# Sliding-window attention in a two-layer trunk: values as stationary weights in two column tiles, probabilities moving, and the later tokens' two key blocks merged by the mask

## The chip, the cores and the metric

The kernel runs on one core of one Trainium2 chip. The metric is the device time of one execution in microseconds. Three runs of the kernel before gave 2478.45, 2480.82 and 2482.11 us, median 2480.82.

The profile names the engines PE (TensorE; PEld are its weight loads), DVE (VectorE), ACT (ScalarE), POOL (GpSimd) and SP (SyncE, which only issues DMAs here). A q behind a name is that engine's instruction queue.

## What is computed

Two layers over 256 tokens of width 2048, in f32. The attention of each layer has 16 query heads of width 64 in 4 groups, one key and value head per group, a window of 128 tokens and a learned sink per head:

```python
scores = jnp.einsum('bnqhgd,bnkhd->bnhgqk', qb, kw).astype(jnp.float32) * scale
q_pos = jnp.arange(BLOCK)[:, None] + BLOCK
k_pos = jnp.arange(2 * BLOCK)[None, :]
diff = q_pos - k_pos
band = (diff >= 0) & (diff < WINDOW)
...
scores = jnp.where(mask, scores, -1e30)
...
probs = jax.nn.softmax(jnp.concatenate([scores, sink], axis=-1), axis=-1)[..., :-1]
out = jnp.einsum('bnhgqk,bnkhd->bnqhgd', probs.astype(v.dtype), vw)
```

With two blocks of 128 tokens, a query of the first block sees keys of its own block up to itself. A query at place q of the second block sees keys 0 to q of its own block and keys q+1 to 127 of the block before: 128 in all, one for each column of a block. The output of the attention goes through `w_attn_branch` (1024 x 2048). Beside it a spatial gating branch, the gates, an output projection and a feed-forward part (width 5632) make up the layer; their large products take most of the time.

## The kernel before

**Large products.** All weights stream from memory in pieces of 256 rows and 512 columns (`Stream`, lines 180 to 230), through five buffers `raw`. ScalarE copies a piece into a rounded part `whi` (line 221), VectorE subtracts to get the rest `wlo` (line 222). Activations are kept the same way as a pair `uh`, `ul`, with features on the partitions. A product is then three matmuls: `whi` by `uh`, `wlo` by `uh`, `whi` by `ul` (lines 309, 310, 311, in `add_product`), each with a 128x128 stationary block of activations and 512 moving columns of weights. For most column pairs (`pair`) a quarter of the rows is done with seven block products for eight, from sums of weights and of activations, which adds work on VectorE (lines 209, 335).

**The order of the work.** TensorE's order is the program's. Small work such as the attention is put between large products: `after(n, fn)` registers a step, `tick()` runs the steps that are due, once per 12 large matmuls. Inside a step the instructions of the other engines are queued behind the latest `wlo` that was issued. VectorE's and ScalarE's order is chosen when the program is built, by a scheduler; it is fixed at run time, and each engine takes its instructions in that order.

**The attention.** In `FIRST_PART` keys and values (`kv`, 256 columns each) and two column halves of queries (`q`, c = 0 and 1, eight heads each, two groups) are projected. `Attention.rotate` normalises and rotates them; `turn` transposes blocks of 32 on VectorE (line 379) and puts them in place by 16 DMAs (line 384), issued for the attention on SP's queue. For each half c, tile of tokens t and group g:

- `scores` (lines 710 to 741): for each row half j, two f32 matmuls of 64 rows into a bank of `ps_at` (line 719); the mask of 0 and -1e30 is added by VectorE (line 723), over 128 columns per head for t = 0 and 256 for t = 1; maximum (727), exponentials on ScalarE (736) with the sums, `den` (738) and its reciprocal `rd` (740).
- `weights`, five ticks later: TensorE transposes the four heads' probabilities `pr` into a bank of `ps_tr`, one per block of keys (748), and ScalarE copies them out as `pT` (750).
- `values`, three ticks later: for each head and block of keys a matmul with `pT` as the stationary 128x128 block and 64 moving columns of values (758). VectorE multiplies the result by `rd` into `att` (762).

After the last group of a half, `transposed` turns `att` on VectorE and SP, and splits it into `uh` and `ul` for the product with `w_attn_branch`.

**Memory.** Most of these tiles are `slot`s: 25 buffers of 4 KB per partition. `pT` and other short-lived tiles are `temp`s (5 buffers). PSUM has four banks for large sums, two (`ps_tr`) for transposes and two (`ps_at`) shared by scores, values and the spatial branch.

Of the kernel before, what the change touches and what calls it, by code (L numbers as in the profile page):

```python
# [8 lines left out]
F32 = mybir.dt.float32  # L9
# [5 lines left out]
P = 128  # L15
# [42 lines left out]
def hybrid_trunk(ctx: ExitStack, tc: tile.TileContext, x, mix_norm, w_in, q_norm, k_norm, sinks,  # L58
# [92 lines left out]
    plans = []  # L151
    for l in range(DEPTH):
        wl = w_in[l]

        def of_in(kind, c):
            o = {"kv": O_KV, "q": 0, "v": O_V, "u": O_U, "gate": O_GATE}[kind] + c * CW
            return wl[:, o:o + CW]

        for f in FIRST_PART[l]:
            plans.append((single if len(f) == 1 else pair)(("in", l), *(of_in(*c) for c in f)))  # L160
        plans += [single(("att", l), w) for w in cols_of(w_attn_branch[l], NCH)]
# [22 lines left out]
    class Stream:  # L184
# [7 lines left out]
        def load(self, upto):  # L192
            while self.asked < min(upto, len(entries)):
                for key, w, h, tag in entries[self.asked]["loads"]:
                    raw = wraw.tile([P, 2, CW], F32, tag=tag, name=nm("raw"), bufs=None if tag == "raw" else 1)
                    src = w[2 * h * P:2 * (h + 1) * P, :].rearrange("(k p) n -> p k n", p=P)
                    if self.raws:
                        self.loaded = nc.sync.dma_start(raw, src)
                    else:
                        for i in range(2):  # L200
                            self.loaded = nc.sync.dma_start(raw[:, i:i + 1], src[:, i:i + 1])
                    self.raws[key] = raw
                self.asked += 1

# [317 lines left out]
    for c in range(NCH):  # L522
# [6 lines left out]
    nc.gpsimd.affine_select(mask[:, :P], mask[:, :P], pattern=[[1, P]], base=0, channel_multiplier=-1,  # L529
                            compare_op=ALU.is_gt, fill=-1e30)  # L530
    nc.gpsimd.affine_select(mask[:, P:], mask[:, P:], pattern=[[-1, P]], base=0, channel_multiplier=1,
                            compare_op=ALU.is_ge, fill=-1e30)
# [100 lines left out]
    class Attention:  # L633


        def __init__(self, pl):
            self.pl = pl
            self.qT = [None] * 2
            self.att = [None] * 2
            self.attT = [None] * 2  # L640
            self.live = {}

        def rotate(self, src, n, rope, outs):

# [64 lines left out]

        def scores(self, t, g):  # L710
            nk = P * (t + 1)
            mk = mask[:, P:] if t == 0 else mask
            snk, nsnk = self.pl.snk, self.pl.nsnk
            pr = slot([P, 2, 2, S], name="pr")
            for j in range(2):
                pscore = ps_at.tile([P, 2, S], F32, tag="at", name=nm("psc"))
                for i in range(2):
# [5 lines left out]
                nc.vector.tensor_tensor(out=pr[:, :, j, :nk], in0=pscore[:, :, :nk],  # L723
                                        in1=mk.unsqueeze(1).to_broadcast([P, 2, nk]), op=ALU.add)
            pr4 = pr.rearrange("p i j k -> p (i j) k")
            mx = tiny(4, "mx")
            nc.vector.tensor_reduce(out=mx, in_=pr4[:, :, :nk], axis=AX.X, op=ALU.max)
            nm_ = tiny(4, "negm")
            nc.vector.scalar_tensor_tensor(out=nm_, in0=mx, scalar=-1.0, in1=nsnk[:, 4 * g:4 * g + 4],
                                           op0=ALU.mult, op1=ALU.min)  # L730
# [2 lines left out]
            nc.scalar.activation(es, es, AF.Exp)  # L733
            den = tiny(4, "den")
            for h in range(4):
                nc.scalar.activation(pr4[:, h, :nk], pr4[:, h, :nk], AF.Exp, bias=nm_[:, h:h + 1],
                                     accum_out=den[:, h:h + 1])
            nc.vector.tensor_tensor(out=den, in0=den, in1=es, op=ALU.add)
            rd = tiny(4, "rd")
            nc.vector.reciprocal(out=rd, in_=den)  # L740
            after(5, lambda: self.weights(t, g, pr4, rd))

        def weights(self, t, g, pr4, rd):
            pT = []
            for kb in range(t + 1):
                pt = ps_tr.tile([P, 4, P], F32, tag="tr", name=nm("ppt"))
                for h in range(4):
                    nc.tensor.transpose(pt[:, h, :], pr4[:, h, kb * P:(kb + 1) * P], ident)  # L748
                pT_ = temp((P, 4, P), "pT")
                nc.scalar.activation(pT_, pt, AF.Copy)  # L750
                pT.append(pT_)
            after(3, lambda: self.values(t, g, pT, rd))

        def values(self, t, g, pT, rd):
            po = ps_at.tile([P, 4, HD], F32, tag="at", name=nm("po"))
            for h in range(4):
                for kb in range(t + 1):
                    nc.tensor.matmul(po[:, h, :], pT[kb][:, h, :],  # L758
                                     self.kv[:, kb, KVW + g * HD:KVW + (g + 1) * HD],
                                     start=kb == 0, stop=kb == t)  # L760
            o = (g % 2) * 256
            nc.vector.tensor_tensor(out=self.att[g // 2][:, t, o:o + 256].rearrange("p (h d) -> p h d", d=HD),
                                    in0=po, in1=rd.unsqueeze(2).to_broadcast([P, 4, HD]), op=ALU.mult)

    class Spatial:

# [236 lines left out]
```

## Time and profile before

| | |
|---|---|
| time of three runs | 2478.45, 2480.82, 2482.11 us |
| span of the profiled execution | 2481.3 us |
| TensorE busy, share of the span | 2465.4 us, 99% |
| VectorE | 1930.1 us, 78% |
| ScalarE | 1430.9 us, 58% |
| granted TensorE clock in the attention's stretches | 1.00 |
| bytes read from memory | 475.27 MB, 192 GB/s over the span |
| attention on TensorE, instructions of scores, transposes, values | 128, 96, 192 |

The page gives busy time per engine, groups of instructions with count, mean time and what ended the idle time before them, and the chain of waits that ended last. Matmuls overlap: a large one is shown as 0.39 us, but the next starts before it ends, so starts are to be compared and not durations. An f32 matmul is recorded as two instructions, a transpose as one.

The attention of layer 0 lies between about 100 and 250 us (first half c = 0 up to about 185), that of layer 1 between about 1340 and 1490 us.

### The profile page before, as it was taken

How to read it: one execution, taken by the hardware profiler on the slowest of the kernel's cores; microseconds unless marked ns; L12 is line 12 of the kernel's file. 1: busy time of each engine (PE TensorE's matmuls, PEld its weight loads, DVE VectorE, ACT ScalarE, POOL GpSimd, SP SyncE). 2: the span in 40 equal slices, each digit the busy share in tenths (PEclk: the TensorE clock that was granted, in tenths of full speed). 3: DMA queues.
4: the chain of work that ended last, by engine and by line, in shares of the span. 5: the costliest groups of instructions: out<-in, count | busy, mean ns of one | idle time of the engine just before them, and what ended most of it. 6: DMA issues, size and time to landing. Idle time of an engine off the chain costs nothing.

```text
span 2481.3 us, 31298 instructions
## 1 busy us (share of the span) xinstructions
PE 2465.4 (99%) x11088; PEld 2028.1 (82%) x11088; DVE 1930.1 (78%) x2261; ACT 1430.9 (58%) x1794; POOL 283.4 (11%) x527
## 2 busy tenths in 40 slices
PE   9999999999999999999999999999999999999999
PEld 7888888888888888888887888888888888888887
DVE  6698676887877787778887986768878777877786
ACT  5567544575655565556655665546655555655564
POOL 3100002231110111001101000021211001110110
PEclk9999999999999999999999999999999999999999
DMA  8565667576666667576747446666757566666664
GB/s 292 192 190 158 215 197 220 184 234 194 217 198 198 212 191 229 171 225 190 228 147 270 147 159 223 207 209 195 224 188 231 185 214 195 217 197 203 211 191 150
DMA packets 275661, 502.54 MB, mean 203 GB/s; under 512 B 26224, under 2 KB 36048, under 8 KB 275504
## 3 DMA queue, kind: packets, MB, share of 16 engines
q1 hardware_dynamic: 259472, 484.25, 61.3%
q0 software_dynamic: 15712, 16.01, 2.2%
q8 instruction: 87, 1.43, 0.2%
q14 instruction: 70, 0.57, 0.1%
q10 hardware_dynamic: 320, 0.27, 0.0%
HBM read 475.27 MB, written 2.10 MB: 192 GB/s over the span
## 4 chain that ended last, share of the span: by engine, by line
PE 90%; DVE 4%; DMA 2%; issue 1%; SPq 1%; ACT 1%; POOL 0%; DVEq 0%; ACTq 0%
PE acc L309 29%; PE acc L311 29%; PE acc L310 29%; DMA raw<-in_w_in_dram 2%; DVE wlo L222 2%; SPq L384 1%; PE po L758 1%; ACT whi L221 1%; DVE raw L209 1%; PE pt L421 1%; PE ppt L748 0%; PE psc L719 0%; DVE box L379 0%; PE psg L836 0%; DVE ul L412 0%
## 5 line engine op out<-in xcount | busy, mean ns | idle before, releaser
L222 DVE TENSOR_TENSOR wlo<-raw,whi 128x1024 fp32r<-128x1024 f32 (+1 forms) x1039 | 1264.8, 1220 | 498.5 <-ACT whi L221 481.3
L221 ACT ACTIVATE whi<-raw 128x1024 fp32r<-128x1024 f32 (+1 forms) x1039 | 1098.0, 1058 | 929.2 <-PE acc L311 749.3
L309 PE MATMUL acc<-whi,uh 128*128 128x512 f32 x3114 | 1218.1, 391 | 2.5 <-ACT uh L407 1.6
L310 PE MATMUL acc<-wlo,uh 128*128 128x512 f32 x3114 | 1212.9, 390 | 1.7 <-DVE wlo L222 1.6
L311 PE MATMUL acc<-whi,ul 128*128 128x512 f32 x3114 | 1212.8, 389 | 0.0
L310 PEld LDWEIGHTS acc<-wlo,uh 128*128 128x128 f32 x3114 | 585.1, 188 | 124.9 <-DVE wlo L222 4.7
L309 PEld LDWEIGHTS acc<-whi,uh 128*128 128x128 f32 x3114 | 585.1, 188 | 123.6 <-ACT uh L407 1.8
L311 PEld LDWEIGHTS acc<-whi,ul 128*128 128x128 f32 x3114 | 584.8, 188 | 122.5
L384 POOL DMA_DIRECT2D tt<-box x480 | 235.1, 497 | 1716.6 <-DVE box L379 835.7
L209 DVE TENSOR_TENSOR raw<-raw,raw 128x1024 f32<-128x1024 f32 x188 | 229.2, 1219 | 1.3
L309 PE MATMUL acc<-whi,sh 128*128 128x512 f32 x376 | 150.6, 401 | 3.7 <-DVE kept L335 2.8
L311 PE MATMUL acc<-whi,sl 128*128 128x512 f32 x376 | 146.7, 390 | 0.0
L310 PE MATMUL acc<-wlo,sh 128*128 128x512 f32 x376 | 146.5, 390 | 0.0
L309 PEld LDWEIGHTS acc<-whi,sh 128*128 128x128 f32 x376 | 70.5, 188 | 30.2 <-issue 12.3
L311 PEld LDWEIGHTS acc<-whi,sl 128*128 128x128 f32 x376 | 70.6, 188 | 15.1
L310 PEld LDWEIGHTS acc<-wlo,sh 128*128 128x128 f32 x376 | 70.7, 188 | 13.1
L335 DVE TENSOR_TENSOR kept<-acc,kept 128x512 f32<-128x512 f32 x94 | 64.1, 682 | 0.0
L338 ACT ACTIVATE acc<-kept 128x512 f32<-128x512 f32 x94 | 54.0, 587 | 7.5 <-DVE kept L335 7.4
L853 DVE SCALAR_TENSOR_TENSOR xs<-acc,xs 128x512 f32<-128x512 f32 (+1 forms) x66 | 41.2, 666 | 7.8 <-PE acc L311 7.8
L942 ACT ACTIVATE hid<-acc,rhalf 128x512 f32<-128x512 f32 x44 | 30.4, 690 | 21.0 <-PE acc L311 21.0
L332 ACT ACTIVATE kept<-acc 128x512 f32<-128x512 f32 x47 | 28.1, 597 | 15.0 <-PE acc L311 15.0
L943 DVE SCALAR_TENSOR_TENSOR hid<-hid,acc 128x512 f32<-128x512 f32 x44 | 29.6, 683 | 8.3 <-ACT hid L942 8.3
(135 smaller groups left out, 878.5 us busy)
## 6 DMA issues: line engine op xcount, KB each, us to landing
raw<-in_w_in_dram SPq DMA_DIRECT2D x239, 512.0 KB, 4.7
raw<-in_w_up_dram SPq DMA_DIRECT2D x176, 512.0 KB, 4.8
raw<-in_w_gate_dram SPq DMA_DIRECT2D x176, 512.0 KB, 4.6
raw<-in_w_down_dram SPq DMA_DIRECT2D x176, 512.0 KB, 4.7
raw<-in_w_out_dram SPq DMA_DIRECT2D x64, 512.0 KB, 4.9
raw<-in_w_attn_branch_dram SPq DMA_DIRECT2D x32, 512.0 KB, 5.4
raw<-in_w_sgu_branch_dram SPq DMA_DIRECT2D x32, 512.0 KB, 4.4
tt<-box POOLq DMA_DIRECT2D x480, 32.0 KB, 4.2
```

What stands on the lines that cost most here:

```text
L209: self.last = nc.vector.tensor_tensor(out=self.raws[d], in0=self.raws[x], in1=self.raws[y], op=ALU.subtract)
L221: nc.scalar.activation(hi[:, i, :], raw[:, i, :], AF.Copy)
L222: self.last = nc.vector.tensor_tensor(out=lo[:, i, :], in0=raw[:, i, :], in1=hi[:, i, :].bitcast(F32), op=ALU.subtract)
L309: nc.tensor.matmul(ps, a, hi[:, kk, :], start=first and kk == 0, stop=False, skip_group_check=True)
L310: nc.tensor.matmul(ps, a, lo[:, kk, :], start=False, stop=False, skip_group_check=True)
L311: nc.tensor.matmul(ps, b, hi[:, kk, :], start=False, stop=kk == 1, skip_group_check=True)
L335: nc.vector.tensor_tensor(out=p.kept[:, int(tag == "P7"), :], in0=a[1], in1=p.kept[:, 1, :], op=ALU.add)
L338: nc.scalar.activation(ps, p.kept[:, t, :], AF.Copy)
L384: queue.dma_start(dst[j * B:(j + 1) * B, i], box[i * B:(i + 1) * B, j])
L853: nc.vector.scalar_tensor_tensor(out=xs[:, t, sl], in0=sums[t][:, i * w:(i + 1) * w], scalar=scale, in1=xs[:, t, sl], op0=ALU.mult, op1=AL ...
L942: nc.scalar.activation(th, g[t], AF.Tanh, scale=norm.rh[t])
L943: nc.vector.scalar_tensor_tensor(out=th, in0=th, scalar=1.0, in1=g[t], op0=ALU.add, op1=ALU.mult)
```

## The change

1. **Values.** One step per half c and tile of tokens t, in place of one per group. The values of a group (128 keys x 64) are the stationary operand; the turned probabilities of the group's four heads (128 keys x 512) move. The two groups of the half write partitions 0 to 63 and 64 to 127 of one bank. The result has features on partitions already, so the turn of `att` is gone: ScalarE copies the bank to `uh`, VectorE subtracts to get `ul`. The pairs `uh`, `ul` are allocated when the queries of the half begin.
2. **Scaling.** `rd` multiplies the probabilities before they are turned, two ticks after the scores.
3. **Second tile of tokens.** The two blocks of scores are merged into one of 128 columns: ScalarE copies the own block's scores, VectorE overwrites those where the mask is set with the block before's. Maximum, exponentials and transposes run over 128 columns per head instead of 256. The values are V0 times all turned probabilities plus (V1 - V0) times those of the own block, which a 0/1 matrix `causal` selects (V0 the block before). Hence `kv`'s first key columns, which are free after the rotation, are overwritten with V1 - V0.

   In the program's names: for t = 1 and k = 0 the stationary operand is the first block's values, for k = 1 the difference.
4. **Attention-branch weights.** The features of the output now lie in another order, so each load of these weights is made by two DMAs of 64 partitions, from rows picked by head.

```diff
+    def rows_of(raw, w, h):
+
+        if w.shape[0] != QW or not any(w is a for a in by_heads):
+            return [(raw, w[2 * h * P:2 * (h + 1) * P, :].rearrange("(k p) n -> p k n", p=P))]
+        rows = w.rearrange("(c a k d) n -> c a d k n", c=2, a=2, d=HD)
+        k = 2 * (h % 2)
+        return [(raw[a * HD:(a + 1) * HD], rows[h // 2, a, :, k:k + 2]) for a in range(2)]
...
-    mask = const.tile([P, S], F32, name="mask")
+    mask = const.tile([P, P], F32, name="mask")
...
+    causal = const.tile([P, P], F32, name="causal")
+    nc.gpsimd.memset(causal, 1.0)
+    nc.gpsimd.affine_select(causal, causal, pattern=[[1, P]], base=0, channel_multiplier=-1, compare_op=ALU.is_ge, fill=0.0)
...
+            after(K_TURN, lambda: nc.vector.tensor_tensor(out=kv[:, 0, :KVW], in0=kv[:, 1, KVW:], in1=kv[:, 0, KVW:],
+                                                          op=ALU.subtract))
...
-            self.att[c] = slot([P, NT, CW], name="att")
+            self.attT[c] = None
+            units = slot([P, 4, S], F32R, "uh"), slot([P, 4, S], F32R, "ul")
...
                     after(n, lambda t=t, g=g: self.scores(t, g))
                     n += Q_STEP
-            after(n + 6, lambda: transposed(self.attT, c, self.att[c], queue=nc.sync))
+                after(n + 3, lambda t=t: self.values(t, c, units))
...
-            pr = slot([P, 2, 2, S], name="pr")
+            if g % 2 == 0:
+                self.pr[t, g // 2] = slot([P, 2, 4, P], name="pr")
+            pr4 = self.pr[t, g // 2][:, g % 2]
...
-                nc.vector.tensor_tensor(out=pr[:, :, j, :nk], in0=pscore[:, :, :nk],
-                                        in1=mk.unsqueeze(1).to_broadcast([P, 2, nk]), op=ALU.add)
+                mk = mask.unsqueeze(1).to_broadcast([P, 2, P])
+                if t == 0:
+                    nc.vector.tensor_tensor(out=pr[:, :, j, :], in0=pscore[:, :, :P], in1=mk, op=ALU.add)
+                else:
+                    nc.scalar.activation(pr[:, :, j, :], pscore[:, :, P:], AF.Copy)
+                    nc.vector.copy_predicated(pr[:, :, j, :], mk.bitcast(mybir.dt.uint32), pscore[:, :, :P])
...
-            after(5, lambda: self.weights(t, g, pr4, rd))
...
+            after(2, lambda: nc.vector.tensor_tensor(out=pr4, in0=pr4, in1=rd.unsqueeze(2).to_broadcast([P, 4, P]),
+                                                     op=ALU.mult))
+            after(5, lambda: self.weights(t, g, pr4))
+
+        def weights(self, t, g, pr4):
+            if g % 2 == 0:
+                self.pT[t, g // 2] = [slot([P, 2, 4, P], name="pT") for _ in range(t + 1)]
+            pT = self.pT[t, g // 2]
+            pt = ps_tr.tile([P, 4, P], F32, tag="tr", name=nm("ppt"))
             for h in range(4):
...
+                nc.tensor.transpose(pt[:, h, :], pr4[:, h, :], ident)
+            nc.scalar.activation(pT[0][:, g % 2], pt, AF.Copy)
+            if t == 1:
+                nc.vector.tensor_tensor(out=pT[1][:, g % 2], in0=pt, in1=causal.unsqueeze(1).to_broadcast([P, 4, P]),
+                                        op=ALU.mult)
+
+        def values(self, t, c, units):
+            po = ps_at.tile([P, 4, P], F32, tag="at", name=nm("po"))
+            pT = self.pT[t, c]
+            for k in range(t + 1):
+                for a in range(2):
+                    v = (1 - k) * KVW + (2 * c + a) * HD
+                    nc.tensor.matmul(po[a * HD:(a + 1) * HD], self.kv[:, 0, v:v + HD], pT[k][:, a],
+                                     start=k == 0, stop=k == t)
+            uh, ul = (x[:, :, t * P:(t + 1) * P] for x in units)
+            nc.scalar.activation(uh, po, AF.Copy)
+            nc.vector.tensor_tensor(out=ul, in0=po, in1=uh.bitcast(F32), op=ALU.subtract)
+            if t == NT - 1:
+                self.attT[c] = units
```

More of the change, by code (lines that the diff above doesn't have):

```diff
@@ L149, in pair @@
         return Plan(key, head, body)
-    plans = []
+    plans, by_heads = [], []
     for l in range(DEPTH):
@@ L160, in hybrid_trunk @@
             plans.append((single if len(f) == 1 else pair)(("in", l), *(of_in(*c) for c in f)))
-        plans += [single(("att", l), w) for w in cols_of(w_attn_branch[l], NCH)]
+        by_heads += cols_of(w_attn_branch[l], NCH)
+        plans += [single(("att", l), w) for w in by_heads[-NCH:]]
         sgu = [single(("sgu", l), w_sgu_branch[l, :, j * CW:(j + 1) * CW]) for j in range(NCH)]
@@ L195, in load @@
                     raw = wraw.tile([P, 2, CW], F32, tag=tag, name=nm("raw"), bufs=None if tag == "raw" else 1)
[L196 to L201, printed above, removed]
+                    for dst, src in rows_of(raw, w, h):
+                        if self.raws:
+                            self.loaded = nc.sync.dma_start(dst, src)
+                        else:
+                            for i in range(2):
+                                self.loaded = nc.sync.dma_start(dst[:, i:i + 1], src[:, i:i + 1])
                     self.raws[key] = raw
@@ L525, in hybrid_trunk @@
     after(10, lambda: norm.unit(WINO, again=True))
-    mask = const.tile([P, S], F32, name="mask")
+    mask = const.tile([P, P], F32, name="mask")
     nc.gpsimd.memset(mask, 0.0)
-    nc.gpsimd.affine_select(mask[:, :P], mask[:, :P], pattern=[[1, P]], base=0, channel_multiplier=-1,
-                            compare_op=ALU.is_gt, fill=-1e30)
-    nc.gpsimd.affine_select(mask[:, P:], mask[:, P:], pattern=[[-1, P]], base=0, channel_multiplier=1,
+    nc.gpsimd.affine_select(mask, mask, pattern=[[-1, P]], base=0, channel_multiplier=1,
                             compare_op=ALU.is_ge, fill=-1e30)
+    causal = const.tile([P, P], F32, name="causal")
+    nc.gpsimd.memset(causal, 1.0)
+    nc.gpsimd.affine_select(causal, causal, pattern=[[1, P]], base=0, channel_multiplier=-1, compare_op=ALU.is_ge, fill=0.0)
     cs = const.tile([P, NT, HD // 2], F32, name="cs")
@@ L638, in __init__ @@
             self.qT = [None] * 2
-            self.att = [None] * 2
             self.attT = [None] * 2
-            self.live = {}
+            self.pr, self.pT = {}, {}
         def rotate(self, src, n, rope, outs):
@@ L711, in scores @@
             nk = P * (t + 1)
-            mk = mask[:, P:] if t == 0 else mask
             snk, nsnk = self.pl.snk, self.pl.nsnk
-            pr = slot([P, 2, 2, S], name="pr")
+            if g % 2 == 0:
+                self.pr[t, g // 2] = slot([P, 2, 4, P], name="pr")
+            pr4 = self.pr[t, g // 2][:, g % 2]
+            pr = pr4.rearrange("p (i j) k -> p i j k", j=2)
             for j in range(2):
@@ L722, in scores @@
                                      start=True, stop=True)
-                nc.vector.tensor_tensor(out=pr[:, :, j, :nk], in0=pscore[:, :, :nk],
-                                        in1=mk.unsqueeze(1).to_broadcast([P, 2, nk]), op=ALU.add)
-            pr4 = pr.rearrange("p i j k -> p (i j) k")
+                mk = mask.unsqueeze(1).to_broadcast([P, 2, P])
+                if t == 0:
+                    nc.vector.tensor_tensor(out=pr[:, :, j, :], in0=pscore[:, :, :P], in1=mk, op=ALU.add)
+                else:
+                    nc.scalar.activation(pr[:, :, j, :], pscore[:, :, P:], AF.Copy)
+                    nc.vector.copy_predicated(pr[:, :, j, :], mk.bitcast(mybir.dt.uint32), pscore[:, :, :P])
             mx = tiny(4, "mx")
-            nc.vector.tensor_reduce(out=mx, in_=pr4[:, :, :nk], axis=AX.X, op=ALU.max)
+            nc.vector.tensor_reduce(out=mx, in_=pr4, axis=AX.X, op=ALU.max)
             nm_ = tiny(4, "negm")
@@ L735, in scores @@
             for h in range(4):
-                nc.scalar.activation(pr4[:, h, :nk], pr4[:, h, :nk], AF.Exp, bias=nm_[:, h:h + 1],
+                nc.scalar.activation(pr4[:, h, :], pr4[:, h, :], AF.Exp, bias=nm_[:, h:h + 1],
                                      accum_out=den[:, h:h + 1])
@@ L740, in scores @@
             nc.vector.reciprocal(out=rd, in_=den)
-            after(5, lambda: self.weights(t, g, pr4, rd))
[L743 to L752, printed above, removed]
@@ L754, in values @@
-        def values(self, t, g, pT, rd):
-            po = ps_at.tile([P, 4, HD], F32, tag="at", name=nm("po"))
-            for h in range(4):
[L757 to L763, printed above, removed]
+            after(2, lambda: nc.vector.tensor_tensor(out=pr4, in0=pr4, in1=rd.unsqueeze(2).to_broadcast([P, 4, P]),
+                                                     op=ALU.mult))
```

## The prediction

> **What bounds the kernel now.** I read the page's busy shares and costliest groups first, then the order of time on TensorE, then TensorE's waits.
>
> ```profile
> PE 2465.4 (99%) x11088; PEld 2028.1 (82%) x11088; DVE 1930.1 (78%) x2261; ACT 1430.9 (58%) x1794; POOL 283.4 (11%) x527
> ...
> L309 PE MATMUL acc<-whi,uh 128*128 128x512 f32 x3114 | 1218.1, 391 | 2.5 <-ACT uh L407 1.6
> ...
> L309 PE MATMUL acc<-whi,sh 128*128 128x512 f32 x376 | 150.6, 401 | 3.7 <-DVE kept L335 2.8
> ```
> ```profile
> 108.05 0.39 PE L310 MATMUL acc<-wlo,uh 128*128 128x512 f32 x1
> ...
> 117.11 0.39 PE L311 MATMUL acc<-whi,ul 128*128 128x512 f32 x1
> ```
>
> Lines 309, 310 and 311 each run 3114 + 376 times, so 10470 large matmuls. The two timeline rows are 40 starts apart: 9.06 / 40 = 0.2265 us each, and 10470 x 0.2265 = 2371 us of the 2481.3 us span. TensorE is the bound; a microsecond taken from it counts, unless it then waits. VectorE is second, and the table by stretches shows where it binds:
>
> ```profile
> 124.00:170.00 46.00, 44.72 (x229) 36.10 (x230) 45.26 (x85) 33.47 (x62) 3.86 (x2) 1.00 0.59 189
> 170.00:250.00 80.00, 80.00 (x416) 66.41 (x415) 69.09 (x117) 53.35 (x96) 2.61 (x3) 1.00 0.55 166
> 1360.00:1400.00 40.00, 38.47 (x189) 31.16 (x190) 38.94 (x76) 26.95 (x50) 2.02 (x2) 1.00 0.51 163
> ```
>
> Columns: stretch, length, then busy time of TensorE, its weight loads, VectorE, ScalarE, GpSimd, then clock (1.00: full), DMA share, GB/s. In the first column half's attention of each layer (rows one and three) VectorE is busy 45.26 of 46 and 38.94 of 40 us, and of the three rows only these show TensorE idle. In the second half (row two) it has room.
>
> **TensorE's part: what goes.** In the chain of waits stand the prices of the attention's blocks:
>
> ```profile
> 163.91 1.73 PE po L758 x16
> ...
> 188.32 0.65 PE psc L719 x8
> ...
> 196.40 0.84 PE po L758 x8
> 204.13 1.07 PE psc L719 x8
> ...
> 236.71 0.88 PE ppt L748 x8
> ...
> 253.04 0.86 PE psg L836 x4
> ```
>
> Columns: start, time on the chain, work. There are 16 value blocks (2 layers, 4 groups, 2 tiles of tokens): 8 of the first tile at 0.84 and 8 of the second at 1.73, together 20.6 us. The second tile's transposes fall from eight to four in 8 blocks: 8 x 0.44 = 3.5 us gone.
>
> **What comes.** Eight value blocks instead of 16, each of a tile of tokens and a column half: 4 instructions for the first tile, 8 for the second (an f32 matmul is recorded as two), 512 moving columns each. No such instruction is in the trace. The nearest is psg: 0.86 / 4 = 0.215 us for 256 columns, so 0.43 for 512. Two column tiles at once do not occur either; the nearest is psc, whose two row halves do: eight instructions of 256 columns take 1.07, not 8 x 0.215 = 1.72. That is four pairs at 0.215, 0.86, and 0.21 over for entering and leaving (at 128 columns 0.65, by the same rule 0.43 + 0.21). By it a new block costs 2 x 0.43 + 0.21 = 1.07 or 4 x 0.43 + 0.21 = 1.93, and eight cost 4 x 3.00 = 12.0. I take this row because it is the same kind of split. Bounds: one tile after the other, 4 x (1.72 + 0.21) + 4 x (3.44 + 0.21) = 22.3; no switch, 10.3. So values save 8.6 (from -1.7 to 10.3), and TensorE's own work falls by 12.1, some 3.0 in each of the four halves.
>
> The Trainium skill, TensorE: Matmul & The Clock Gate (Part 3: Packing small matmuls, Measured speedup vs the span model), gives three column tiles 2.38 times the speed of one, not 3; at that efficiency (an estimate from that page) two would give 1.6, the blocks 20.6 / 1.6 + 1.7 = 14.6 and the saving 6.0 instead of 8.6. Nothing in this trace shows a column tile, so I keep the row.
>
> **The other engines.**
>
> ```profile
> L723 DVE TENSOR_TENSOR pr<-psc,mask 128x512 f32<-128x512 f32 x16 | 10.8, 680 | 1.4 <-PE psc L719 1.4
> L727 DVE TENSOR_REDUCE mx<-pr 128x4 f32<-128x1024 f32 x8 | 9.7, 1208 | 0.1
> L762 DVE TENSOR_TENSOR att<-po,rd 128x256 f32<-128x256 f32 x16 | 6.6, 413 | 0.0
> L723 DVE TENSOR_TENSOR pr<-psc,mask 128x256 f32<-128x256 f32 x16 | 6.1, 415 | 1.4 <-PE psc L719 1.4
> L379 DVE STREAM_TRANSPOSE box<-att 128x512 f32<-128x512 f32 x8 | 5.6, 703 | 0.0
> L727 DVE TENSOR_REDUCE mx<-pr 128x4 f32<-128x512 f32 x8 | 5.4, 672 | 0.0
> ```
>
> VectorE, per layer. Gone: 8 wide mask additions (5.4), the wide halves of 4 maxima (4 x 0.536 = 2.1), 8 scalings of the output (3.3), 4 turns of att (2.8): 13.6. New: 8 predicated copies of 128x256 (by the narrow addition 0.415, 3.3; as a bound 0.68, 5.4), 8 multiplications of probabilities by rd over 128x512 (0.68, 5.4), 4 causal products (0.68, 2.7), one difference of values (0.42): 11.8. (Splitting the result into uh and ul stays, four times 0.68.) It gets 1.8 lighter, or 0.3 heavier at the bound; but what goes last (the turns) lay in the roomy stretch, and the multiplications land in the full one, so I count no relief there. ScalarE swaps 4 evictions and 16 longer exponentials per layer for 8 copies of half a bank; it is 58% busy, and I cost this at nothing.
>
> ```profile
> SPq L198 <- DVE wlo L222: 1656.1, 707, 9.7
> ...
> raw<-in_w_attn_branch_dram SPq DMA_DIRECT2D x32, 512.0 KB, 5.4
> ```
>
> SP loses the 64 DMAs that turn att and issues 32 more (each load of attention-branch weights becomes two of 64 partitions). Its queue stands 1656 us waiting for a weight buffer (first row), which hides them; without it, 16 issues per layer would delay loads that land in 5.4 us. I cost it at nothing.
>
> **The new wait.** Now rd is needed only when the output is scaled, long after the transposes. In the change the transposes take probabilities already multiplied by rd, so TensorE stands, with every large matmul behind it in order, until VectorE has reached that product. How late is rd already?
>
> ```profile
> 133.41 0.15 DVE L738 TENSOR_TENSOR den<-den,es 128x4 f32<-128x4 f32 x1
> ...
> 135.83 0.17 DVE L740 RECIPROCAL rd<-den 128x4 f32<-128x4 f32 x1
> ...
> 172.38 0.15 DVE L738 TENSOR_TENSOR den<-den,es 128x4 f32<-128x4 f32 x1
> ...
> 175.18 0.16 DVE L740 RECIPROCAL rd<-den 128x4 f32<-128x4 f32 x1
> ...
> 1394.43 0.15 DVE L738 TENSOR_TENSOR den<-den,es 128x4 f32<-128x4 f32 x1
> ...
> 1396.24 0.17 DVE L740 RECIPROCAL rd<-den 128x4 f32<-128x4 f32 x1
> ```
> ```profile
> 135.98 0.66 PE L748 MATMUL ppt<-ident,pr 128*128 128x128 f32 x4
> ...
> 170.41 1.09 PE L748 MATMUL ppt<-ident,pr 128*128 128x128 f32 x8
> ...
> 1395.65 1.09 PE L748 MATMUL ppt<-ident,pr 128*128 128x128 f32 x8
> ```
>
> These are three steps of the first halves, rd above and the transposes of the same probabilities below. Layer 0's last one has rd 4.8 us after its transposes began, layer 1's 0.6 after. And a step that depends on its predecessor doesn't follow at once: den to rd takes 2.42, 2.80 and 1.81 us, mean 2.3, since other work stands between them. So I put the product's start 2.3 behind rd's and its end 0.7 later: 178.2 in layer 0 and 1399.2 in layer 1, and TensorE is 7.8 and 3.6 us behind today's time there. (The step at 135.98 is 2.9 late; that is contained in the 7.8.) Savings made before these points are swallowed, for VectorE sets the time; those after them come off. Layer 0: own transposes 0.44, one value block of 1.73 less the new 1.93, and the second half 3.0, together 3.2. Layer 1, where it is one step earlier: two times 0.44, two of 1.73 less 1.93, and 3.0, together 5.4. Sum: 7.8 - 3.2 + 3.6 - 5.4 = +2.8.
>
> For the hop of 2.3 the bounds are 0.2 (straight behind rd: 2.1 less at each point, sum -1.4) and 4.4, which negm takes behind mx in this stretch (2.1 more at each, sum +7.0):
>
> ```profile
> 159.32 1.21 DVE L727 TENSOR_REDUCE mx<-pr 128x4 f32<-128x1024 f32 x1
> ...
> 163.74 0.15 DVE L729 SCALAR_TENSOR_TENSOR negm<-mx,nsnk 128x4 f32<-128x4 f32 x1
> ```
>
> **A second one.** The bank of the value product is cleared by two steps (ScalarE, then VectorE), not one, before the next scores get it two ticks later. In the full stretches this is one more hop; I add 1 us in each first half (between 0 and the hop of 2.3), 2 in all.
>
> **Sum.** 2481.3 + 2.8 + 2 = 2486.1, about 2486. The three runs lie from 2478.45 to 2482.11 with a median of 2480.82, so the span stands for them to 0.5 us. Own range of this forecast: 2476 (both waits at their lower bounds and part of the steps on time) to 2494.
>
> **Rivals.**
>
> *The saving survives (faster).* The order on VectorE is chosen anew when the program is built, and the second tile's chain loses work: maxima 0.54 shorter, the second halves of its scores narrower. If the products end before their transposes, TensorE keeps its 12.1, less some 3 in which VectorE holds it in the full stretches: 2481.3 - 9 = 2472. For it: 99% of the span is TensorE, and in the second half every product is in time. Against it: the late rds above. It decides from about 5 us less lateness of rd in layer 0.
>
> *Column tiles run in turn (slower).* The values then cost 22.3, not 12.0: 2486 + 10 = 2496. Against it: psc's 1.07.
>
> *A buffer runs short (slower).* The output's high and low parts are taken from the large-slot pool when the queries begin, a hundred microseconds and more before they are written, and probabilities turned take slots too. If an eviction of a gate waits for one, a PSUM bank stays full. I can bound it only by the longest stalls of today, TensorE's idle 1.3 and 1.5 us in the full stretches (46.00 - 44.72, 40.00 - 38.47), doubled in both layers: about +6, 2492. No wait in the trace names a slot, which speaks against it.
>
> **Numbers.** Forecast 0.50, saving survives 0.30, tiles in turn 0.10, buffers 0.10. What this kernel's measurement can tell from no change is about 0.2%, 5 us. The forecast's own mass: 0.03 faster, 0.15 same, 0.32 slower; the first rival 0.29 faster, 0.01 same; the two others slower, but for 0.01. Together faster 0.32, same 0.17, slower 0.51. The range for 8 in 10 goes from 2469, which holds nearly all of the first rival, to 2497, which holds the second.
>
> **What would show it.** Right: TensorE idle before ppt, released by VectorE's write of pr, some microseconds in layer 0's first half and fewer in layer 1's, none in the second halves; value blocks near 1.1 and 1.9 us; 64 transposes instead of 96; VectorE's share in the first halves still at 95% or more. Wrong: no idle time before ppt (then the first rival); value blocks of 1.9 and 3.7 (tiles in turn); idle time before score blocks released by ul (the second wait larger than I took it); or new waits of large matmuls for gates or whi.

## The result, and the profile after

The changed kernel takes 2484.17 us (median of 11 runs, 2482.86 to 2489.35), the kernel before, run beside it, 2479.90 (2478.45 to 2483.03). The ratio is 1.0019, 95% interval 1.0012 to 1.0027: slower by about 4.5 us. Forecast was 2486. The profiled execution has a span of 2487.6 us and is the slowest of the 11 runs, so its sums run some 5 us above the median.

First the page's busy times and the groups that answer to those of before (line numbers have moved: the large products are now lines 318 to 320, the transposes 768, the values 780).

```profile
PE 2460.6 (99%) x10912; PEld 2010.6 (81%) x10912; DVE 1930.4 (78%) x2263; ACT 1429.7 (57%) x1802; POOL 282.0 (11%) x528
```
```profile
L768 PE MATMUL ppt<-ident,pr 128*128 128x128 f32 x64 | 11.6, 310 | 15.6 <-DVE pr L758 9.3 <-ACT sq L809 4.9 <-DVE wsT L629 1.4
L758 DVE TENSOR_TENSOR pr<-pr,rd 128x512 f32<-128x512 f32 x16 | 10.9, 683 | 0.2
...
L742 DVE COPY_PREDICATED pr<-mask,psc 128x256 f32<-128x256 uint32 x16 | 6.5, 438 | 0.0
```

In the kernel before, the group of the transposes was:

```profile
L748 PE MATMUL ppt<-ident,pr 128*128 128x128 f32 x96 | 13.8, 280 | 2.5 <-DVE wsT L619 2.5
```

The 64 transposes have 15.6 us of idle time before them; it was 2.5 us for 96. Of it 1.4 us, and before the change all 2.5, wait for a tile of the spatial branch, `wsT`; the other 14.2 us are new. That idle time ends with VectorE's product of probabilities and rd (line 758). The 4.9 put down to ScalarE are the same case: that product ended at 1404.75 + 0.68, in the same moment as a step of ScalarE, and the transposes began at 1405.58.

The order of time on TensorE and VectorE, at the step that the prediction put at 178.2:

```profile
173.15 0.72 PE L733 MATMUL psc<-kT,qT 64*128 64x128 f32 x8
178.94 1.09 PE L768 MATMUL ppt<-ident,pr 128*128 128x128 f32 x4 [5.07 <-DVE pr L758]
179.68 0.77 PE L318 MATMUL acc<-whi,uh 128*128 128x512 f32 x1
180.25 0.63 PE L319 MATMUL acc<-wlo,uh 128*128 128x512 f32 x1
180.68 0.63 PE L320 MATMUL acc<-whi,ul 128*128 128x512 f32 x1
...
184.52 0.40 PE L320 MATMUL acc<-whi,ul 128*128 128x512 f32 x1
184.76 0.39 PE L318 MATMUL acc<-whi,uh 128*128 128x512 f32 x1
```
```profile
174.59 0.15 DVE L755 TENSOR_TENSOR den<-den,es 128x4 f32<-128x4 f32 x1
...
175.86 0.17 DVE L757 RECIPROCAL rd<-den 128x4 f32<-128x4 f32 x1
...
176.59 1.21 DVE L231 TENSOR_TENSOR wlo<-raw,whi 128x1024 fp32r<-128x1024 f32 x1
...
178.12 0.67 DVE L758 TENSOR_TENSOR pr<-pr,rd 128x512 f32<-128x512 f32 x1
```

TensorE stands 5.07 us for the product. What the prediction had not: behind the wait large matmuls start 0.43 us apart instead of 0.23, for some 5 us. The table by stretches shows the reason in its clock column (third from the right, ahead of DMA share and GB/s; before it busy times as in the prediction's table):

```profile
173.50:179.00 5.50, 0.43 (x9) 0.27 (x6) 5.50 (x14) 2.84 (x5) 0.00 (x0) 0.88 0.62 204
179.00:187.50 8.50, 8.50 (x29) 6.89 (x30) 4.32 (x15) 3.40 (x11) 1.01 (x1) 0.68 0.20 61
1400.50:1405.50 5.00, 0.18 (x2) 0.00 (x0) 5.00 (x10) 3.92 (x8) 0.00 (x0) 0.76 0.78 230
1405.50:1413.50 8.00, 7.92 (x28) 6.57 (x29) 5.10 (x12) 4.35 (x12) 0.00 (x0) 0.73 0.19 64
```

The waits of 4.25, 5.07 and 4.89 us (layer 0 twice, layer 1 once) each bring a stretch at half clock, called a dip below. It begins inside the wait, 3.5, 3.8 and 2.4 us after TensorE fell idle, and lasts 6.83 us (136.72 to 143.55, 177.68 to 184.51, 1403.07 to 1409.90: the clock column shows 0.50 there). In this execution 31 large matmuls behind the three waits come late, most of them 0.427 us apart in place of 0.227, and lose 6.6 us together (2.54, 2.34 and 1.74; a first count, which stands in an expectation below, had 29 and 5.8).

The new blocks, in the chain of waits (start, time, work):

```profile
222.63 1.01 PE po L780 x4
...
244.62 0.44 PE ppt L768 x4
...
254.59 1.87 PE po L780 x8
```

They cost what the prediction took from the row halves: 1.01 and 1.87 against 1.07 and 1.93. So two column tiles with different moving data run side by side (one after the other, eight instructions of 0.43 would take 3.44). The sum for the profiled execution: -12.1 for TensorE's work, +13.1 of waits before the transposes (15.6 less the 2.5 of before), +6.6 for the large matmuls at half clock and +1.0 for the three groups of transposes that run at half clock too (each 0.74 us from its start to the next matmul's, 0.41 elsewhere) give +8.6. The span is 6.3 longer, or 8.2 without TensorE's first 15 us, which went 1.9 faster in it (by the starts of the same large matmul in both traces; the execution of the kernel before has a dip of 3.41 us there, from 7.67). So the sum is 0.4 us too large.

### The profile page after: what moved, and what is told of

It is laid out like the page before. It is cut to its first block, busy times and chain, and to the rows that moved or that the text cites. A ratio compares the mean times of both kernels' runs of the same rounds, so it can differ in the third digit from the quotient of the medians.

```text
span 2487.6 us, 30931 instructions
## 1 busy us (share of the span) xinstructions
PE 2460.6 (99%) x10912; PEld 2010.6 (81%) x10912; DVE 1930.4 (78%) x2263; ACT 1429.7 (57%) x1802; POOL 282.0 (11%) x528
## 4 chain that ended last, share of the span: by engine, by line
PE 90%; DVE 5%; DMA 2%; issue 1%; ACT 1%; SPq 0%; POOL 0%; DVEq 0%; ACTq 0%
PE acc L318 30%; PE acc L319 29%; PE acc L320 29%; DVE wlo L231 2%; DMA raw<-in_w_in_dram 2%; DVE raw L218 1%; ACT whi L230 1%; PE pt L430 1%; PE po L780 0%; PE ppt L768 0%; PE psc L733 0%; PE psg L859 0%; DVE ul L421 0%; DVE box L388 0%; DVE kept L344 0%
## 5 line engine op out<-in xcount | busy, mean ns | idle before, releaser
L319 PEld LDWEIGHTS acc<-wlo,sh 128*128 128x128 f32 x376 | 70.6, 188 | 13.1
```

Of the source, the lines that this page charges most:

```text
L319: nc.tensor.matmul(ps, a, lo[:, kk, :], start=False, stop=False, skip_group_check=True)
```

## The experiments

All are timed beside the kernel before on the same chip; ratios are to that kernel.

### Without the product, and with the product aside

```diff
 # e2_no_scale
-            after(2, lambda: nc.vector.tensor_tensor(out=pr4, in0=pr4, in1=rd.unsqueeze(2).to_broadcast([P, 4, P]),
-                                                     op=ALU.mult))
 # e5_product_aside
+            aside = temp((P, 4, P), "aside")
-            after(2, lambda: nc.vector.tensor_tensor(out=pr4, in0=pr4, ...
+            after(2, lambda: nc.vector.tensor_tensor(out=aside, in0=pr4, ...
```

> The changed kernel without the product of probabilities and rd; rd is still computed, the output stays unnormalised. Theory: the transposes wait for the exponentials alone, which ended 4 to 11 us before the product in the three slow steps; no wait over 1 us, clock 1.00, 2467 to 2472. Rival (VectorE's load is what counts): VectorE is 5.4 us per layer lighter and the time falls by no more than that, to 2476 or above; a second rival, that other parts of the change cost the time (loads in halves, buffers), expects 2480 or above.

> The changed kernel whose product of probabilities and rd goes to a tile that nothing reads; the transposes take the unscaled probabilities, so VectorE has all its work and the wait is gone (the output is unnormalised). Theory (it is the wait that costs, not VectorE's load): 2468 to 2474, no wait before the transposes, clock 1.00. Rival (VectorE's load in its full stretches): the 12.7 us between this kernel without the product and the kernel before are given back, 2478 to 2484, with waits for wlo.

Without the product: 2468.77 us, ratio 0.9952 (0.9939 to 0.9964). With the product computed into a tile that nobody reads: 2469.89, ratio 0.9956 (0.9943 to 0.9968). All of TensorE's saving, 11.5 us, appears while VectorE does all its work. By the two ratios the load costs about 1 us, which is less than their intervals resolve. The wait costs the rest: the changed kernel (1.0019) is 15.6 us slower than this one. What TensorE still waits for with the product aside:

```profile
PE acc L318 <- DVE kept L344: 4.1, 5, 1.5
PE acc L319 <- DVE wlo L231: 2.1, 5, 0.6
PE ppt L769 <- DVE wsT L629: 1.5, 1, 1.5
```

The lines name who waits, for whom, the total, the number and the longest: no single wait is over 1.5 us, and none is for `pr`. The granted clock is 1.00 in the attention's stretches. The rival of VectorE's load is out. This run also carries the halved loads, the early `uh` and `ul` and the merge, so together they take some 0.6 us of the 12.1, within an interval of 3 us to either side.

### The wait put into the kernel before

```diff
 # kernel before, e4_old_scaled_first
+            after(2, lambda: nc.vector.tensor_tensor(out=pr4[:, :, :nk], in0=pr4[:, :, :nk],
+                                                     in1=rd.unsqueeze(2).to_broadcast([P, 4, nk]), op=ALU.mult))
             after(5, lambda: self.weights(t, g, pr4, rd))
...
-            nc.vector.tensor_tensor(out=self.att[g // 2][:, t, o:o + 256]..., in0=po, in1=rd..., op=ALU.mult)
+            nc.vector.tensor_copy(self.att[g // 2][:, t, o:o + 256]..., po)
```

> The kernel before with only the scaling moved: probabilities are multiplied by rd two ticks after the scores, ahead of the transposes, and the output is copied out unscaled. Theory: the new wait alone does the harm, so it appears here too, in layer 0's three later first-half steps and layer 1's third, with halved clock behind waits over 4 us: 2487 to 2500. Rival (the harm is in the column tiles, the merged mask or the halved loads): 2479 to 2484, as VectorE only gets 8 wide products more per layer.

2496.04 us, ratio 1.0061 (1.0048 to 1.0073): moving the scaling alone costs the old kernel 14.6 us, with waits of the same kind:

```profile
PE ppt L750 <- DVE pr L741: 7.3, 2, 5.5
PE ppt L750 <- DVE ve L805: 5.3, 1, 5.3
```

The second line names `ve`, a small step of VectorE's queue that ended last before the release; it stands before the transposes of layer 0's third step (5.34 us of idle time there, 5.47 in layer 1's third). The forecast of this run had a wait before layer 0's last step too; there is none. The move also gives VectorE 15 us more work in both layers together (the copy of the output takes as long as its scaling did), so this run doesn't part the order from the load; e5 does. Together they show that part 2 of the change costs more than the other parts save.

### Where the product stands in VectorE's order

```diff
 # e3_inline
-            after(2, lambda: nc.vector.tensor_tensor(out=pr4, in0=pr4, ...
+            nc.vector.tensor_tensor(out=pr4, in0=pr4, ...
```

> The changed kernel with the product issued right behind rd in the same step, not two ticks later. Theory: the hop from rd to the product, 1.3 to 4.3 us in the three slow steps, shrinks to about 1; layer 0's first long wait vanishes, the second and layer 1's shrink to about 3 us, and the clock is halved at most once: 2474 to 2481. Rival (the hop is set by the order on VectorE, not by the tick): within 2 us of the changed kernel, 2482 to 2486.

2487.61 us, ratio 1.0024 (1.0014 to 1.0034): no gain, and above the rival's range too. The trace says why:

```profile
150.94 0.17 DVE L757 RECIPROCAL rd<-den 128x4 f32<-128x4 f32 x1
...
155.25 0.68 DVE L758 TENSOR_TENSOR pr<-pr,rd 128x512 f32<-128x512 f32 x1
```

These are layer 0's third step, which has the longest hop of the first half but no long wait. The product stands 4.3 us behind rd as in the changed kernel (151.82 and 156.13): five other steps, two of them over a microsecond long, still come between. In the three steps that wait longest in the changed kernel the hop is 1.20, 2.26 and 2.13 us in both kernels. It shrinks elsewhere, as behind layer 0's fifth step (from 4.41 to 0.21), where nothing waits for it. So in the full stretches the scheduler's order sets the hop and not the tick. The waits are 2.65, 5.11, 1.76 and 4.90 us, and all four are followed by a dip of the clock, against three in the changed kernel.

```diff
 # e7_on_gpsimd
-            nc.vector.tensor_tensor(out=den, in0=den, in1=es, op=ALU.add)
+            nc.gpsimd.tensor_tensor(out=den, in0=den, in1=es, op=ALU.add)
-            nc.vector.reciprocal(out=rd, in_=den)
+            nc.gpsimd.tensor_tensor(out=rd, in0=den, in1=neg_one[:, :4], op=ALU.pow)
...
+            nc.gpsimd.tensor_tensor(out=pr4, in0=pr4, in1=rd.unsqueeze(2).to_broadcast([P, 4, P]), op=ALU.mult)
```

> The changed kernel with the sum den, its reciprocal (as a power of -1) and the product on GpSimd, so that none of the three stands behind other work on VectorE. Theory (the lateness is VectorE's queue, several microseconds from the exponentials' end to the product's end): GpSimd, 11% busy, does the three in about 4 us behind the exponentials, and the transposes then wait about 1 us at most; with 5.4 us of VectorE's work per layer gone too: 2466 to 2473, below the kernel before by 8 to 14. Rival (the product is late because its scores' chain is late, or GpSimd is slow on 512 columns or slows VectorE): 2478 or above.

2489.24 us, ratio 1.0033 (1.0021 to 1.0045): the rival, by both of its causes. GpSimd's order of time at layer 0's last step of the first half, and at layer 1's third:

```profile
168.76 1.15 POOL L757 TENSOR_TENSOR den<-den,es 128x4 f32<-128x4 f32 x1 [11.39 <-ACT es L752]
169.98 1.01 POOL L759 TENSOR_TENSOR rd<-den,neg_one 128x4 f32<-128x4 f32 x1
171.07 2.08 POOL L760 TENSOR_TENSOR pr<-pr,rd 128x512 f32<-128x512 f32 x1
```
```profile
1394.35 0.20 POOL L757 TENSOR_TENSOR den<-den,es 128x4 f32<-128x4 f32 x1 [1.67 <-ACT es L752]
1394.63 1.01 POOL L759 TENSOR_TENSOR rd<-den,neg_one 128x4 f32<-128x4 f32 x1
1395.72 6.25 POOL L760 TENSOR_TENSOR pr<-pr,rd 128x512 f32<-128x512 f32 x1
```

In layer 0 the three follow one another closely, 4.4 us in all, but the first starts at 168.76: GpSimd had been idle for 11.39 us until the chain of scores got to it. Taking the last three steps off VectorE does not help where the steps before them are late. In layer 1 the sum is early (1394.35; TensorE falls idle at 1398.00), but there the product itself takes 6.25 us, and TensorE waits 4.02 us for its end. What slowed it was not tried. The waits before the transposes for GpSimd's product are 11.6 us.

### More time before the transposes

```diff
 # e1_late (e8_late7: 7 and n + 4)
-            after(5, lambda: self.weights(t, g, pr4))
+            after(8, lambda: self.weights(t, g, pr4))
...
-                after(n + 3, lambda t=t: self.values(t, c, units))
+                after(n + 6, lambda t=t: self.values(t, c, units))
```

> The changed kernel with its transposes eight ticks after the scores instead of five, the values still three ticks behind them. Theory (the transposes wait for the product of probabilities and rd, and the long waits then halve the clock): the product of layer 0's last first-half step ended 22 us after its scores, eight ticks are about 22 us, so no wait over 1 us is left before the transposes and the clock stays at 1.00; TensorE keeps most of its 12 us: 2468 to 2473. Rival (VectorE sets the pace of the first halves whatever waits for it): the same microseconds come back as waits of large matmuls for wlo in the first halves: 2479 to 2484.

> The changed kernel with the transposes seven ticks after the scores and the values two ticks behind them, so that the values come ahead of the next scores again. With eight and three, the values stood behind the next scores and waited 5.7 us for a bank that the merge had not read yet. Theory (that bank wait was the only new cost of the later transposes): the waits for the bank vanish, 2468 to 2474. Rival (each place trades one wait of the full stretches for another): some of it stays, as waits for the merge, wlo or pT, 2476 to 2482.

Eight ticks: 2480.21 us, ratio 0.9997 (0.9989 to 1.0006). Seven: 2479.22, ratio 0.9991 (0.9982 to 0.9999). Both beat the changed kernel, and both miss the theory's range; the rivals were right in time, though it is not `wlo` that TensorE waits for but banks. With eight, the values come behind the next scores and wait for a bank that the merge has not read; with seven, the next scores wait until the values' bank has been cleared by ScalarE and then VectorE:

```profile
PE po L780 <- DVE pr L742: 5.7, 4, 3.4
PE acc L318 <- DVE negm L746: 2.1, 1, 2.1
```
```profile
PE psc L733 <- DVE ul L784: 4.4, 3, 2.7
...
PE ppt L768 <- DVE pr L758: 2.4, 2, 2.2
```

Scores and values share two banks, `ps_at`. So the values' bank was moved to the two of the transposes:

```diff
 # e9_late8_tr: 8 and n + 6; e10_late7_tr: 7 and n + 5; both with
-            po = ps_at.tile([P, 4, P], F32, tag="at", name=nm("po"))
+            po = ps_tr.tile([P, 4, P], F32, tag="tr", name=nm("po"))
```

> The changed kernel with transposes eight ticks behind the scores, values three ticks behind the transposes, and the values' bank taken from the two banks of the transposes, so that scores and values no longer share banks. Theory (what was left at eight ticks was the bank: 5.7 us of waits for the merge, 2.1 for negm behind it, and a dip of the clock): no wait over 1.5 us near the attention, clock 1.00, 2468 to 2474. Rival (the first halves are held by VectorE's order, so the time shows up at the next place): 2476 to 2481, with waits for wlo, pT or kept.

> The same with seven ticks to the transposes and three more to the values. Theory: at seven ticks the product was late twice, by 2.4 us in all, in layer 1; the 4.4 us of waits of scores for ul are gone with the banks apart: 2470 to 2475. Rival: as above, 2476 to 2481.

2474.26 us, ratio 0.9972 (0.9961 to 0.9984), and 2473.28, ratio 0.9970 (0.9959 to 0.9981). These beat both kernels: the kernel before by 7 to 8 us, the changed one, by the ratios, by about 12. The bank waits are gone. With eight ticks it just misses the theory's range, as the wait behind `negm` (2.2) and one for a gate (1.3) stayed. With seven, the time lies in the theory's range, though two waits for the product stayed, each followed by a dip:

```profile
PE ppt L768 <- DVE pr L758: 6.1, 2, 3.3
```

### The clock behind a wait

```diff
 # e6_filled, e11_filled_right
+            if (self.pl.l, t, g) in ((0, 0, 1), (0, 1, 1), (1, 1, 0)):      # e6: (0, 1, 0) in place of (0, 0, 1)
+                for _ in range(4):
+                    nc.tensor.matmul(pt.rearrange("p h q -> p (h q)"), ident, xs[:, 0, :CW], start=True, stop=True)
             for h in range(4):
                 nc.tensor.transpose(pt[:, h, :], pr4[:, h, :], ident)
```

> The changed kernel with four f32 matmuls of 512 columns (1.7 us by the psg row, 3.4 us as eight recorded instructions) put ahead of the transposes in the three steps that waited 4 to 5 us; the transposes overwrite their result. Theory (each of these waits halves TensorE's clock for 6.8 us, 3.4 us lost): the work fits into the waits, the idle time left is 1 to 2 us, the clock stays at 1.00, and the time falls though work was added, by 3 to 10 us, to 2474 to 2481. Rival (the clock's dips cost nothing of the end, or come from something else than the idle time): unchanged or up to 3 us longer, 2484 to 2488.

> The changed kernel with the four f32 matmuls of 512 columns ahead of the transposes in the three steps that waited 4 to 5 us: layer 0's second and last of the first half, layer 1's third. (e6_filled had one of the three in layer 0's third step, which had no wait, and left the second's.) Theory (the long waits halve the clock behind them): idle time left 0.5 to 2 us in each, clock 1.00 behind all three, the 29 slow matmuls and their 5.8 us gone: 2477 to 2480, 4 to 7 below the changed kernel. Rival (the dips cost nothing of the end, since VectorE would hold TensorE anyway): 2483 to 2486.

With the filling at the three waits: 2482.81 us, ratio 1.0007 (0.9998 to 1.0016), beside 1.0019 (1.0012 to 1.0027) without it. The trace did what the theory said:

```profile
136.00:146.00 10.00, 10.00 (x45) 7.57 (x43) 7.74 (x23) 5.62 (x15) 1.01 (x1) 1.00 0.19 54
177.00:186.00 9.00, 9.00 (x41) 7.47 (x40) 6.71 (x20) 5.35 (x13) 1.01 (x1) 1.00 0.33 107
1403.00:1411.00 8.00, 8.00 (x36) 6.37 (x34) 6.92 (x20) 4.77 (x12) 1.01 (x1) 1.00 0.43 130
```

The clock is full behind all three places (the third column from the right), and 10.3 us of work by the psg row (3 x 8 x 0.43) were added without making the kernel slower. But the time fell by about 3 us in the ratio, less than the 4 to 7 expected, and the two intervals overlap; 2482.81 lies between the ranges of theory and rival. So the filling shows that the idle time brings the dips; what they cost in a usual run is open. The mean granted clock of a whole run gives an upper bound: it is 0.997 in most runs of the changed kernel and 0.999 with the filling, and 0.002 of 2483 us is about 5 us, which includes half clock while nothing runs. The runs of the changed kernel point to a cost above nothing: the two with the lowest clock (0.996 and 0.995) took 2489.35 and 2488.52 us, the nine others (0.997 and 0.998) 2482.86 to 2485.72.

e6 had one filling at layer 0's third step, which had no wait, and none at the second: 2481.51 us, ratio 1.0002 (0.9993 to 1.0011), just above the theory's range. The wait left unfilled was 2.70 us and a dip followed it; no wait for the last step's product was left. What the filling at the place without a wait cost can't be read from this run.

### The halved loads by themselves

```diff
 # kernel before, e12_old_halved_loads
+                    if self.raws and w.shape[0] == QW:
+                        for a in range(2):
+                            self.loaded = nc.sync.dma_start(raw[a * HD:(a + 1) * HD], src[a * HD:(a + 1) * HD])
```

> The kernel before with the loads of both branch weights (attention and spatial, 64 in all) each made by two DMAs of 64 partitions; nothing else changes. Theory (a load in halves is hidden behind the wait for its buffer): the same as before within 1 us, landing about as late as in the changed kernel, 5.7 us. Rival (twice the DMAs on SP's queue or slower halves delay whi): 2 us or more above the kernel before, with waits of large matmuls for whi in the branch products.

2485.96 us, ratio 1.0020 (1.0012 to 1.0029): the rival. DMA issues and SP's order of time:

```profile
raw<-in_w_attn_branch_dram SPq DMA_DIRECT2D x64, 256.0 KB, 7.4
```
```profile
1527.00 20.75 SPq L199 DMA_DIRECT2D raw<-in_w_attn_branch_dram  x21
1547.86 11.84 SPq L387 DMA_DIRECT2D tt<-box  x16
1559.74 7.46 SPq L199 DMA_DIRECT2D raw<-in_w_attn_branch_dram  x11
```

The loads of the attention branch land after 7.4 us, not 5.4, and stand behind 16 DMAs of a turn of the spatial branch (11.84 us). At 1563 us TensorE runs out of weights (1.52 us of idle time), and its clock falls behind it. The changed kernel halves only the 32 loads of the attention branch. They land after 5.7 us there and stand behind the same turn (16 DMAs at 1552.84, 11.14 us), and no such wait appears. What this queue no longer has there are the 64 DMAs that turned `att`, of which e12 issues 16 from 1499.66, ahead of these loads. That these make the room was not tried by itself.

## Why the prediction was right

**TensorE's work, -12.1.** Right. Value blocks 1.01 and 1.87 for 1.07 and 1.93; the kernel with the product aside runs 11.5 us under the kernel before. "Tiles in turn" (2496) is out.

**The new wait.** Right in its place and mechanism: layer 0's first half, then layer 1's third step, none in the second halves. The product of layer 0's last step was put at 178.2 and ended at 178.79. That this is so close is in part luck: the profiled execution ran 1.9 us ahead from its start, so counted from there the product came 2.5 us later than put. In layer 1 it ended at 1405.43, not 1399.2; TensorE came to this layer's attention some 8 us later already (the same large matmul starts at 1302.05, and at 1293.94 before the change), which the sum by differences left out of the absolute time. The waits for the product add up to 14.2 us. The hop behind rd, put at 2.3, was 1.2 in layer 0's second step (135.46 to 136.66) and 2.3 and 2.1 in the two others that waited (175.86 to 178.12 and 1402.62 to 1404.75). It was 4.3 in layer 0's third (151.82 to 156.13), where TensorE arrived just behind the product.

**VectorE's share.** One sign came out only in part. During the waits VectorE is busy throughout (5.50 of 5.50 and 5.00 of 5.00 us in the table above), and in layer 1's stretch from 1366 to 1406 it is busy 39.74 of 40 us. But in layer 0 from 124 to 170 it is busy 39.49 of 46 us, or 86%, where 95% or more was asked for. Behind the waits, with the clock at half for most of the stretch, it is busy only 4.32 of 8.50 us (the second row).

**The clock.** Missed. The prediction took TensorE's price behind a wait to be that before it. 6.6 us in the profiled execution, up to about 5 in a usual run, are from matmuls at half clock. The Trainium skill has the rule (TensorE: Matmul & The Clock Gate, "What's actually happening": after an idle window of about 3.4 us the clock is halved), and the waits of 4.25 and 5.07 us agree with it; shorter ones here go beyond it (last section). The failed step is the one that let a wait cost its own length and no more.

**The second wait (the bank), +2.** Mis-sized: in the changed kernel scores never waited for `ul`. A likely reason is that the product's wait comes earlier in the same stretch and gives VectorE the time: with that wait gone, scores wait 0.5 us for `ul` in e2 and 1.1 in e5, and 4.4 with the transposes at seven ticks (e8).

**The loads, at nothing.** Right for the changed kernel, but the reason given does not hold by itself. The prediction named the queue's wait for buffers; e12 has much the same wait (1599.5 us behind `wlo`, for 1656.1) and is 4.6 us slower, with twice as many halved loads.

**Slots.** In the changed kernel no large matmul waits for a gate, which the rival would have shown.

**The sum.** The forecast was +4.8 on its starting span, the measured medians differ by 4.3. The product's lateness was taken from rows of the same steps, and that part was earned. That the total came out within 1 us is luck: the clock, which it lacked, and the bank, which it had too much of, partly made up for each other.

## What to carry to other kernels

Before a scaling or another cheap step is moved ahead of TensorE's work, look at when the old trace has its input ready, and count the hop in the other engine's queue: here a step whose load costs about 1 us (e5 beside e2) brought some 15 us of waits and dips (the changed kernel beside e5). A saving on a saturated engine is only had if the new order leaves the time between steps (here two more ticks and separate banks: -7.7 us instead of +4.3). And price a wait of TensorE with what the clock does after it.

## What the runs showed of the hardware

Dips of the clock follow shorter waits than I had thought. The stretches at half clock lasted 3.4 or 6.8 us in the traces. They came with all waits of over 3.1 us and with some of 1.5 to 2.9 (e12: 1.52; e3: 1.76 and 2.65; e9: 2.19; e6: 2.70; e8: 2.71; e10: 2.84), while the kernel before had one of 2.48 at 1358 us without any.

What tells these apart is where the wait falls. Within each trace the dips begin whole multiples of 3.41 us apart: in the changed kernel at 136.72, 177.68 and 1403.07, which is 12 and 359 such pieces. Cut the time into these pieces, and leave out TensorE's first 15 us. Then every piece at full clock in which TensorE was idle for 1.97 us or more was followed by a dip, and none with 1.71 or less; of two between, one was (1.76, e3) and one was not (1.79, e7). The wait of 2.48 us in the kernel before lies across the end of a piece, with 1.19 us in one and 1.29 in the next. The one of 1.52 in e12 shares its piece with part of a second wait, 2.15 us in all.

A predicated copy of 128x256 from PSUM took 438 ns, as a masked addition of that size (415); the ScalarE copy before it 377. GpSimd's product of 128x512 took 1645 ns on the mean (median 1252, the longest of the 16 6245), VectorE's 683.
